# Order edges for inverses and output blocks, output blocks loaded a wave ahead, and a row of ones written once, in a two-layer RWKV-7 / attention backbone

## The chip, the cores and the metric

One NeuronCore of a Trainium2 chip. The metric is the device time of one execution in microseconds, lower is better. The kernel before took 2486.58 us in the median of 3 runs (2473.8 to 2494.9). All data is float32; products that need its precision are made of two or three matmuls on a rounded high part and a low part.

## The reference, cut to what matters

Two layers work on 1280 tokens (256 of context, 1024 latent) of width 1024. A layer projects the modulated stream into three groups of heads, lets each group mix the tokens, multiplies with a gate, projects back and normalises. Group A is a recurrence over the tokens that runs in both directions:

```python
def _rwkv7_step(S, inp):
    r, w, k, v, kk, b = inp
    sa = jnp.einsum('bhvk,bhk->bhv', S, kk)
    S = S * w[:, :, None, :] - sa[..., None] * b[:, :, None, :] + v[..., None] * k[:, :, None, :]
    return S, jnp.einsum('bhvk,bhk->bhv', S, r)
...
    yn = ((ys - mu) * lax.rsqrt(var + GN_EPS)).reshape(T, B, RWKV_W) * gn_g + gn_b
    bonus = jnp.sum(jnp.sum(r[:, :, None] * kd * r_k, axis=-1, keepdims=True), axis=2) * v
```

Groups B (grouped-query attention) and C (attention in a window of a grid) are softmax attention:

```python
        s = jnp.einsum('bqgrd,bsgd->bgrqs', qi, keys).astype(jnp.float32)
        p = jax.nn.softmax(s, axis=-1).astype(vals.dtype)
        return jnp.einsum('bgrqs,bsgd->bqgrd', p, vals)
...
    y_l = jnp.concatenate([yr_l * jax.nn.silu(rg_l), ya_l * jax.nn.silu(ag_l),
                           yn_l * jax.nn.silu(ng_l)], axis=-1) @ w_out
```

## The kernel before, in words

**Stages of a layer.** `layer_proj` projects; `rwkv` (L512, group A) is started in its middle; `attention` (L808, groups B and C) and `out_weights` / `out_proj` follow. They are traced one after the other, but the order in which an engine carries them out is drawn up when the kernel is built: `TileContext` is opened with `schedule_with_timeline_sim=True`, and its planner fills each engine's queue from the traced instructions by their order of tracing and by its own idea of when each becomes ready. On the chip each queue is then followed as it stands. So the attention, traced later, fills what the recurrence leaves free. `follow` (L803) gives the planner an edge without a semaphore: an instruction may not stand ahead of another one. It is used for one matmul in `weigh` (L924).

**The recurrence by waves.** The 1280 tokens make `NW` = 10 waves of 128, a wave 4 steps of 32 tokens, both directions at once. For each wave there are six stages of preparation and one chain:

- `p` `wave_pre` (L545): loads r, kk, kd, bd from DRAM (L556, tags `ldr` with 2 buffers, `ldkk`, `ldkd`, `ldbd` with 1), decays (tiles `th`, `iv`, `lp`), products into `G` and `kb`.
- `g` `wave_gram` (L602): Gram matrices (L610) and masks (L615). `l` `wave_low` (L590): their lower triangles go to DRAM `ls_d` (L594) and come back spread out as `lin` (L600).
- `i` `wave_inv` (L631): two copies from `lin` to `nn` (L634, L635), 15 steps of two dependent VectorE operations each (L643, L645), then through DRAM `inv_d` (L656, L660) into `di`. `k` `wave_kt` (L618): transposes. `m` `wave_merge` (L663): two rounds of small matmuls (L674) and `tt` (L679).
- `wave_chain` (L682): per step loads of v into one of three `X` tiles (L696), clearing of X (L698), matmuls (L703), a copy (L706), matmuls (L714), copies (L720), matmuls into the state (L724) and the update that writes the next X (L729). The step's output (`out_step`, L742, tile `py`) is put off to behind the next step's copy. After a wave its outputs go to DRAM `y_d` (L749).

`out_block` (L755) takes 128 tokens once both directions have written them: 7 loads (L761 y, L764 yb in four pieces, L765, L766), the sum on GpSimd (L767), normalisation on VectorE, ScalarE and GpSimd (L769 to L776), three transposes into PSUM (L780, tile `pso`), scale and shift (L782), bonus (L785), gate (L786), store to `yg_d` (L787), which `out_proj` reads (L1130). y and yb share the two buffers of `ldr`; the odd block of a pair takes `th` and `iv` for its other two tiles, the even one `ldkd` and `ldbd`. PSUM of the tag `pp` (two buffers) holds `psz`, `pcu`, `gt`, `kt`, `mg`, `py` and `pso` alike.

The order of tracing is the loop at L790: `wave_chain(w)`, then stages i, k of wave w+2, p, g, l of w+3, m of w+2, then output blocks: from wave 6 on the pair (11 - w, w), and in layer 0 the pair (0, 1) after wave 1.

**Attention.** `load_k` (L833) loads a head's keys twice (L830), rounds them (`k1`, L837), takes the rest on GpSimd into rows 0 to 63 of `k2` (L838), and writes a row of ones into row 64 (L839), which the correction matmul (L937) uses to add the row of maxima. It is called 6 times a layer. Scores (L867) give maxima (L869, L871, L874); then scores again (L936, L937), exponentials (L943, L946), sums (L950, L955) and the product with v (L921).

Of the kernel before, what the change touches and what calls it, by code (L numbers as in the profile page):

```python
# [8 lines left out]
F32 = mybir.dt.float32  # L9
F32R = mybir.dt.float32r  # L10
AF = mybir.ActivationFunctionType
ALU = mybir.AluOpType
AX = mybir.AxisListType
# [4 lines left out]
T = 1280  # L18
# [25 lines left out]
def body(tc, a):  # L44
    nc = tc.nc
# [10 lines left out]
    ident = cload("ident", [128, 128], nc.gpsimd)  # L56
# [444 lines left out]


# [9 lines left out]
    def rwkv(l, lay):  # L512
        last = l == DEPTH - 1
# [8 lines left out]
        z = bank[:, 0:384].rearrange("p (d c v) -> p d c v", d=2, c=3)  # L522
# [20 lines left out]
        pend = []  # L543

# [86 lines left out]
        def wave_inv(w):  # L631

            nn = r2.tile([128, 16, 16], F32, tag="nn", name="nn")
            nc.vector.tensor_copy(nn[0:64], lin[0:64].rearrange("p i t -> p t i"))  # L634
            nc.vector.tensor_copy(nn[64:128], lin[64:128])  # L635
# [46 lines left out]
        def wave_chain(w):  # L682
# [5 lines left out]
            for j in range(4):  # L688
# [3 lines left out]
                for d in range(2):  # L692
                    t0 = 128 * wave_block(w, d) + 32 * jc[d]
                    for p in range(2):
                        q, qs = QV[d][p], QSA[d][p]
                        nc.sync.dma_start(out=x[q:q + 32, d, :, p, :],  # L696
                                          in_=vt_d[t0:t0 + 32, :].rearrange("t (c e v) -> t c e v", c=3, e=2)[:, :, p, :])
                        nc.gpsimd.memset(x[qs:qs + 32, d, :, p, :], 0.0)  # L698
# [27 lines left out]
                if s < 4 * NW - 1:  # L726
                    for p in range(2):
                        o = slice(64 * p, 64 * p + 64)
                        nc.vector.tensor_tensor(out=xn[o, :, :, p, :], in0=z[o], in1=dcj(dc[o, 0, j], j), op=ALU.mult)  # L729
# [22 lines left out]
        def dcj(v, j):  # L752
            return bass.AP(tensor=v.tensor, offset=v.offset, ap=[v.ap[0], [21 - 6 * j, 2], [1, 3], [0, 64]])

        def out_block(b, odd):  # L755
            t4 = ("th", "iv") if odd else ("ldkd", "ldbd")
            y, yb = (r3.tile([128, 6, 64], F32, tag=t, name="yo", bufs=2) for t in ("ldr", "ldr"))
            bv, gt = (r3.tile([128, 3, 128], F32, tag=t, name="go", bufs=1) for t in t4)
            hv = lambda t: t.rearrange("p h v -> p (h v)")
# [7 lines left out]
            nc.gpsimd.tensor_tensor(out=y, in0=y, in1=yb, op=ALU.add)  # L767
            sm = r3.tile([128, 2, 6], F32, tag="sm", name="sm")
            nc.vector.tensor_reduce(out=sm[:, 0], in_=y, op=ALU.add, axis=AX.X)  # L769
# [19 lines left out]
        stages = dict(p=wave_pre, g=wave_gram, l=wave_low, i=wave_inv, k=wave_kt, m=wave_merge)  # L789
        for w in range(-3, NW):  # L790
            if w >= 0:
                wave_chain(w)
            for c in "ikpglm":
                v = w + (2 if c in "ikm" else 3)
                if 0 <= v < NW:
                    stages[c](v)
            for i, b in enumerate((11 - w, w) if w > 5 else (0, 1) if w == 1 and not last else ()):
                out_block(b, i)
        for f in pend:
            f()  # L800
        es.close()

    def follow(ins, prev):  # L803

        tc.add_manual_dep(ins.ins, prev.ins.name, mybir.DependencyInfo(mybir.DependencyClass.NoSync, mybir.DependencyReason.DATA), reason="order")


    def attention(l):  # L808
# [13 lines left out]
        nl = [0]  # L822

# [9 lines left out]
        def load_k(h):  # L833
            sg_ = dup(k_d[h])
            k1 = ap2.tile([128, T], F32R, tag="k1", name="k1")
            k2 = ap2.tile([65, T], F32R, tag="k2", name="k2")
            nc.scalar.copy(k1, sg_)  # L837
            nc.gpsimd.tensor_tensor(out=k2[0:64, :], in0=sg_[0:64, :], in1=k1[0:64, :], op=ALU.subtract)  # L838
            nc.vector.tensor_scalar(out=k2[64:65, :], in0=sg_[64:65, :], scalar1=0.0, scalar2=1.0, op0=ALU.mult, op1=ALU.add)  # L839
            return k1, k2  # L840
# [551 lines left out]
```

## Time and profile before

| | |
|---|---|
| median of 3 runs | 2486.58 us |
| the profiled execution | 2487.74 us |
| its span, first to last instruction | 2485.9 us |
| TensorE busy | 2207.0 us (89%) |
| VectorE busy | 1644.2 us (66%) |
| GpSimd busy | 1183.7 us (48%) |
| ScalarE busy | 1004.3 us (40%) |
| mean granted TensorE clock | 0.936 |
| DMA | 298.17 MB, mean 120 GB/s |

Engines in the profile: PE is TensorE's matmuls, PEld its weight loads, DVE VectorE, ACT ScalarE, POOL GpSimd; SPq is the queue of SyncE, which issues nearly all DMAs. L12 is line 12 of the kernel. In a timeline a row has the start (us), the duration, engine, line, operation, out<-in, and in brackets the engine's idle time before it and what ended it. In a row of waits stand the one that waited, what it waited for, the sum in us, the number of times and the longest. A row of busy times of a stretch has, behind its length, the busy time and the number of instructions of PE, PEld, DVE, ACT and POOL, the granted clock (1 is full speed), the DMA share and GB/s. TensorE's busy time is modelled at its ends, and at a lower clock the same work shows as more busy time.

### The profile page before, as it was taken

The numbers are of one execution on the slowest core, as the hardware profiler recorded it, in microseconds if no ns is written. First come the engines' busy times: TensorE is split into PE (matmuls) and PEld (weight loads), VectorE is DVE, ScalarE is ACT, GpSimd is POOL, SyncE is SP. The second block draws the span as 40 slices with busy tenths as digits, with TensorE's granted clock in tenths as the row PEclk, the third lists the DMA queues.
The fourth block names the chain that finished last, engine by engine and source line by source line (L and its number), as shares of the span: only waits on it lengthen the run. The fifth ranks groups of instructions, "written<-read, shape, count | busy, mean of one in ns | idle before, by whom it ended". The sixth has DMA issues, their size and how long they took to land.

```text
span 2485.9 us, 57805 instructions
## 1 busy us (share of the span) xinstructions
PE 2207.0 (89%) x22616; PEld 1648.8 (66%) x22616; DVE 1644.2 (66%) x3071; ACT 1004.3 (40%) x2186; POOL 1183.7 (48%) x1438
## 2 busy tenths in 40 slices
PE   6999999996898888889899999999868889999797
PEld 3777898774455555545797777787645656555497
DVE  5686433545867778767487796624568878877746
ACT  3333413334453545445233434214344545554522
POOL 3464425335454545344345365433455655645432
PEclk9999999996898989899999999999978989999899
DMA  7344334446554444334332455335564544332332
GB/s 273 114 155 165 119 90 118 124 109 145 129 119 111 96 98 114 101 89 140 110 100 80 140 168 181 110 91 122 132 138 112 122 106 111 96 81 67 115 111 92
DMA packets 448241, 298.17 MB, mean 120 GB/s; under 512 B 249600, under 2 KB 395880, under 8 KB 446944
## 3 DMA queue, kind: packets, MB, share of 16 engines
q1 hardware_dynamic: 439936, 281.71, 41.6%
q0 software_dynamic: 7392, 10.28, 1.5%
q8 instruction: 178, 2.92, 0.5%
q10 hardware_dynamic: 640, 2.49, 0.4%
q14 instruction: 95, 0.78, 0.1%
HBM read 198.37 MB, written 91.79 MB: 117 GB/s over the span
## 4 chain that ended last, share of the span: by engine, by line
PE 43%; DVE 22%; DMA 15%; issue 7%; ACT 5%; POOL 4%; SPq 4%; DVEq 0%; POOLq 0%; ACTq 0%
PE pj L204 5%; PE pj L203 5%; PE pj L205 5%; PE y L921 3%; DMA yf<-yg_d 2%; PE sm L867 2%; DVE G L615 2%; DMA ls_d<-G 2%; PE st L936 2%; DVE tmp L643 2%; DVE mx L869 2%; PE st L937 2%; DVE e L645 2%; PE ch L724 1%; DMA lin<-ls_d 1%
## 5 line engine op out<-in xcount | busy, mean ns | idle before, releaser
L204 PE MATMUL pj<-hlo,wh 128*128 128x512 f32 (+1 forms) x1072 | 402.0, 375 | 12.0 <-DVE hlo L480 7.3
L203 PE MATMUL pj<-hhi,wh 128*128 128x512 f32 (+1 forms) x1072 | 402.2, 377 | 9.1 <-ACT qr L348 5.2
L205 PE MATMUL pj<-hhi,wl 128*128 128x512 f32 (+1 forms) x1072 | 400.0, 374 | 0.2 <-POOL wl L169 0.2
L204 PEld LDWEIGHTS pj<-hlo,wh 128*128 128x128 f32 x1072 | 204.9, 191 | 54.3 <-DVE hlo L480 7.5
L203 PEld LDWEIGHTS pj<-hhi,wh 128*128 128x128 f32 x1072 | 204.0, 191 | 53.6 <-issue 6.8
L169 POOL TENSOR_TENSOR wl<-wf,wh 128x512 fp32r<-128x512 f32 x104 | 142.2, 1372 | 203.6 <-ACT wh L168 188.7
L869 DVE TENSOR_REDUCE mx<-sm 128x1 f32<-128x512 f32 (+1 forms) x372 | 198.9, 553 | 56.6 <-PE sm L867 54.9
L205 PEld LDWEIGHTS pj<-hhi,wl 128*128 128x128 f32 x1072 | 204.7, 191 | 38.1 <-issue 3.2
L943 ACT ACTIVATE pt<-st 128x512 f32<-128x512 f32 (+1 forms) x292 | 165.6, 582 | 144.2 <-PE st L937 141.6
L921 PE MATMUL y<-pt,v 128*64 128x256 f32 (+1 forms) x1392 | 220.0, 408 | 1.3 <-ACT pt L946 1.3
L867 PE MATMUL sm<-k,q 128*128 128x256 f32 (+2 forms) x436 | 169.1, 425 | 26.2 <-DVE mx L869 14.2
L936 PE MATMUL st<-q,k 128*128 128x512 f32 (+3 forms) x376 | 169.0, 452 | 24.0 <-ACT pt L943 8.0
L1159 PE MATMUL pj<-yh,wh 128*128 128x256 f32 x576 | 162.7, 291 | 8.1 <-ACT yh L1133 5.0
L1160 PE MATMUL pj<-yl,wh 128*128 128x256 f32 x576 | 165.5, 290 | 0.9 <-POOL yl L1134 0.8
L1161 PE MATMUL pj<-yh,wl 128*128 128x256 f32 x576 | 162.9, 287 | 0.0
L921 PEld LDWEIGHTS y<-pt,v 128*64 128x64 f32 x1392 | 96.6, 146 | 93.0 <-issue 64.5
L950 POOL TENSOR_TENSOR acc<-acc,pt 128x512 f32<-128x512 f32 x80 | 105.9, 1324 | 95.1 <-ACT pt L943 94.7
L937 PE MATMUL st<-q,k 65*128 65x512 f32 (+3 forms) x376 | 149.3, 400 | 1.1 <-ACT q L881 1.1
L867 PEld LDWEIGHTS sm<-k,q 128*128 128x128 f32 x436 | 82.4, 202 | 92.5 <-DVE mx L869 29.1
L615 DVE TENSOR_TENSOR G<-gt,msk 64x192 f32<-64x192 f32 (+1 forms) x320 | 110.4, 345 | 36.0 <-PE gt L610 24.8
L698 POOL MEMSET X<- 32x192 f32 x320 | 81.7, 255 | 102.2 <-PE py L742 75.7
L950 DVE TENSOR_TENSOR acc<-acc,pt 128x512 f32<-128x512 f32 x112 | 114.7, 1034 | 16.9 <-ACT pt L943 14.9
(276 smaller groups left out, 5124.8 us busy)
## 6 DMA issues: line engine op xcount, KB each, us to landing
wf<-win SPq DMA_DIRECT2D x104, 256.0 KB
wm<-wmod SPq DMA_DIRECT2D x32, 512.0 KB
yf<-yg_d SPq DMA_DIRECT2D x72, 128.0 KB
wt<-wm SPq DMA_DIRECT2D x8, 1024.0 KB
gate_d<-o SPq DMA_DIRECT2D x32, 256.0 KB
wf<-wout SPq DMA_DIRECT2D x16, 512.0 KB
ldkk<-rw_d SPq DMA_DIRECT2D x40, 192.0 KB
ldkd<-rw_d SPq DMA_DIRECT2D x40, 192.0 KB
```

The source lines that it names most:

```text
L203: nc.tensor.matmul(out=ps[:, :n], lhsT=wh, rhs=hhi[:, k, t0:t0 + n], start=(k == 0), stop=False)
L204: nc.tensor.matmul(out=ps[:, :n], lhsT=wh, rhs=hlo[:, k, t0:t0 + n], start=False, stop=False)
L205: nc.tensor.matmul(out=ps[:, :n], lhsT=wl, rhs=hhi[:, k, t0:t0 + n], start=False, stop=(k == KT - 1))
L867: nc.tensor.matmul(out=sp_[:, :o], lhsT=q[0][:, qc:qc + 128], rhs=k[0][:, c0:c0 + o], start=True, stop=True)
L869: nc.vector.tensor_reduce(out=mx[:, n_:n_ + 1], in_=sp_[:, :o], op=ALU.max, axis=AX.X)
L921: mm = nc.tensor.matmul(out=y[64 * i:64 * i + 64, a0:a1], lhsT=v[:, t, :], rhs=pt[:, p0:p0 + a1 - a0], start=start, stop=stop and at == le ...
L936: nc.tensor.matmul(out=o, lhsT=k[0][:, 128 * t:128 * t + 128], rhs=q[0][:, qa:qb], start=True, stop=False)
L937: mm = nc.tensor.matmul(out=o, lhsT=k[1][0:65, 128 * t:128 * t + 128], rhs=q[1][0:65, qa:qb], start=False, stop=True)
L943: nc.scalar.activation(out=pt[:, :w], in_=sp_[:, :w], func=AF.Exp)
L950: eng.tensor_tensor(out=acc[i][:, :w], in0=sums[i][:, :w], in1=pt[:, :w], op=ALU.add)
L1160: nc.tensor.matmul(out=p_, lhsT=wh[m][:, k], rhs=yl, start=False, stop=False)
L1161: nc.tensor.matmul(out=p_, lhsT=wl[m][:, k], rhs=yh, start=False, stop=(x_ == KT - 1))
```

## The change

Three things, in the same launch with the same arithmetic:

1. Each chain notes its second step's update on VectorE and its last clearing of X on GpSimd (`mark`). The two first copies of each inverse (VectorE) and the first GpSimd and first VectorE operation of each output block get an edge, by `follow`, behind the note of the chain traced last.
2. `out_block` is split into `out_load` and `out_block`. Loads are traced at the end of a wave's round, their compute in the next round, between `wave_chain` and the stages. The odd block of a pair has y and yb in the buffers of `ldkk` and `lp`. The blocks 0 and 1 of layer 0 load one at a time, after waves 1 and 2; the last pair of a layer computes after the loop.
3. The two `k2` tiles are taken once per layer from the pool without rotation, and their rows of ones are written there, from the constant `ident`; `load_k` alternates between them and writes rows 0 to 63 alone.

```diff
+        mark = {}
+
+        def behind(ins, eng):
+
+            if eng in mark:
+                follow(ins, mark[eng])
...
-            nc.vector.tensor_copy(nn[0:64], lin[0:64].rearrange("p i t -> p t i"))
-            nc.vector.tensor_copy(nn[64:128], lin[64:128])
+            behind(nc.vector.tensor_copy(nn[0:64], lin[0:64].rearrange("p i t -> p t i")), "v")
+            behind(nc.vector.tensor_copy(nn[64:128], lin[64:128]), "v")
...
-                        nc.gpsimd.memset(x[qs:qs + 32, d, :, p, :], 0.0)
+                        ms = nc.gpsimd.memset(x[qs:qs + 32, d, :, p, :], 0.0)
...
-                        nc.vector.tensor_tensor(out=xn[o, :, :, p, :], in0=z[o], in1=dcj(dc[o, 0, j], j), op=ALU.mult)
+                        up = nc.vector.tensor_tensor(out=xn[o, :, :, p, :], in0=z[o], in1=dcj(dc[o, 0, j], j), op=ALU.mult)
+                    if j == 1:
+                        mark.update(v=up, g=ms)
...
-        def out_block(b, odd):
+        def out_load(b, odd):
             t4 = ("th", "iv") if odd else ("ldkd", "ldbd")
-            y, yb = (r3.tile([128, 6, 64], F32, tag=t, name="yo", bufs=2) for t in ("ldr", "ldr"))
+            if odd:
+                y, yb = r3.tile([128, 6, 64], F32, tag="ldkk", name="yo", bufs=1), r2.tile([128, 6, 64], F32, tag="lp", name="yo")
+            else:
+                y, yb = (r3.tile([128, 6, 64], F32, tag="ldr", name="yo", bufs=2) for _ in range(2))
...
-            nc.gpsimd.tensor_tensor(out=y, in0=y, in1=yb, op=ALU.add)
+            return ts_, y, yb, bv, gt
+
+        def out_block(ts_, y, yb, bv, gt):
+            behind(nc.gpsimd.tensor_tensor(out=y, in0=y, in1=yb, op=ALU.add), "g")
             sm = r3.tile([128, 2, 6], F32, tag="sm", name="sm")
-            nc.vector.tensor_reduce(out=sm[:, 0], in_=y, op=ALU.add, axis=AX.X)
+            behind(nc.vector.tensor_reduce(out=sm[:, 0], in_=y, op=ALU.add, axis=AX.X), "v")
...
+        waiting, loaded = [], []
         for w in range(-3, NW):
             if w >= 0:
                 wave_chain(w)
+            for f in loaded:
+                out_block(*f)
+            loaded = []
             for c in "ikpglm":
                 v = w + (2 if c in "ikm" else 3)
                 if 0 <= v < NW:
                     stages[c](v)
-            for i, b in enumerate((11 - w, w) if w > 5 else (0, 1) if w == 1 and not last else ()):
-                out_block(b, i)
+            waiting += (11 - w, w) if w > 5 else (0, 1) if w == 1 and not last else ()
+            for i in range(2 if w > 5 else 1):
+                if waiting:
+                    loaded.append(out_load(waiting.pop(0), i))
         for f in pend:
             f()
+        for f in loaded:
+            out_block(*f)
         es.close()
...
+        k2s = [ap1.tile([65, T], F32R, tag=f"k2{i}", name=f"k2{i}") for i in range(2)]
+        for z in k2s:
+            nc.vector.tensor_scalar(out=z[64:65, :], in0=ident[64:65, 0:64].unsqueeze(2).to_broadcast([1, 64, 20]), scalar1=0.0, scalar2=1.0, op0=ALU.mult, op1=ALU.add)
+        nk = [0]
...
-            k2 = ap2.tile([65, T], F32R, tag="k2", name="k2")
+            k2 = k2s[nk[0] % 2]
+            nk[0] += 1
...
-            nc.vector.tensor_scalar(out=k2[64:65, :], in0=sg_[64:65, :], scalar1=0.0, scalar2=1.0, op0=ALU.mult, op1=ALU.add)
```

More of the change, by code (lines that the diff above doesn't have):

```diff
@@ L500, in lowrank, with follow @@
         return dict(zw=zw, aw=aw)
+    def follow(ins, prev):
+        tc.add_manual_dep(ins.ins, prev.ins.name, mybir.DependencyInfo(mybir.DependencyClass.NoSync, mybir.DependencyReason.DATA), reason="order")
     QSA = ((32 * 3, 32 * 1), (32 * 2, 32 * 0))
@@ L753, in dcj @@
             return bass.AP(tensor=v.tensor, offset=v.offset, ap=[v.ap[0], [21 - 6 * j, 2], [1, 3], [0, 64]])
-        def out_block(b, odd):
+        hv = lambda t: t.rearrange("p h v -> p (h v)")
+        def out_load(b, odd):
             t4 = ("th", "iv") if odd else ("ldkd", "ldbd")
-            y, yb = (r3.tile([128, 6, 64], F32, tag=t, name="yo", bufs=2) for t in ("ldr", "ldr"))
+            if odd:
+                y, yb = r3.tile([128, 6, 64], F32, tag="ldkk", name="yo", bufs=1), r2.tile([128, 6, 64], F32, tag="lp", name="yo")
+            else:
+                y, yb = (r3.tile([128, 6, 64], F32, tag="ldr", name="yo", bufs=2) for _ in range(2))
             bv, gt = (r3.tile([128, 3, 128], F32, tag=t, name="go", bufs=1) for t in t4)
-            hv = lambda t: t.rearrange("p h v -> p (h v)")
             ts_ = slice(128 * b, 128 * b + 128)
@@ L796, in rwkv @@
                     stages[c](v)
-            for i, b in enumerate((11 - w, w) if w > 5 else (0, 1) if w == 1 and not last else ()):
-                out_block(b, i)
+            waiting += (11 - w, w) if w > 5 else (0, 1) if w == 1 and not last else ()
+            for i in range(2 if w > 5 else 1):
+                if waiting:
+                    loaded.append(out_load(waiting.pop(0), i))
         for f in pend:
             f()
+        for f in loaded:
+            out_block(*f)
         es.close()
-    def follow(ins, prev):
-        tc.add_manual_dep(ins.ins, prev.ins.name, mybir.DependencyInfo(mybir.DependencyClass.NoSync, mybir.DependencyReason.DATA), reason="order")
     def attention(l):
```

## The prediction

> **What bounds the kernel now.** The views were read in this order: the page's totals, the busy times by stage, the timelines of single engines where the recurrence stands still, the waits.
>
> ```profile
> span 2485.9 us, 57805 instructions
> 600.00:1197.00 597.00, 515.48 (x6995) 321.87 (x6996) 448.60 (x1039) 290.08 (x698) 294.33 (x373) 0.91 0.44 111
> 1800.00:2359.00 559.00, 478.33 (x6935) 306.55 (x6935) 439.85 (x1026) 275.26 (x641) 305.00 (x385) 0.91 0.44 106
> ```
>
> The span is 2485.9 us; the profiled execution as a whole took 2487.74 us, and the sum below is made against that. It is 1.2 us above the median of the three runs, 2486.58 us, which spread from 2473.8 to 2494.9; so a measurement of this kernel can tell about 1% (25 us) from no change. The second and third rows are the stretches, 597 and 559 us long, in which the recurrence and the attention share the engines; the columns are the length, the busy time of TensorE, its weight loads, VectorE, ScalarE and GpSimd, then the granted clock. TensorE is busy for 86% of both, at a mean clock of 0.91. That is where a change of order can win: TensorE's idle time and its lost clock there. Below, the "full-clock work" of a stretch is TensorE's busy time times the granted clock, divided by the length.
>
> Three single steps of the chain are far too long. For each of them the rows show the matmuls of the third step (L724), the next transposes of an output block (L780) and the update that ends the step (L729); for the first also the output step (L742). The columns are start, duration, engine and line, and at the end the idle time before and what ended it.
>
> ```profile
> 628.16 0.91 PE L724 MATMUL ch<-X,S 128*64 128x64 f32 x22
> 685.13 0.55 PE L780 MATMUL pso<-c_ident,yo 128*128 128x128 f32 x3
> 685.61 0.54 PE L742 MATMUL py<-X,G 128*32 128x64 f32 x24
> 686.25 1.14 DVE L729 TENSOR_TENSOR X<-ch,dc 64x384 f32<-64x384 f32 x2 [1.34 <-PE py L742]
> 984.88 0.92 PE L724 MATMUL ch<-X,S 128*64 128x64 f32 x24 [1.98 <-DVE nm L874]
> 1029.85 0.84 PE L780 MATMUL pso<-c_ident,yo 128*128 128x128 f32 x3
> 1031.57 1.14 DVE L729 TENSOR_TENSOR X<-ch,dc 64x384 f32<-64x384 f32 x2 [0.79 <-PE py L742]
> 2176.33 0.92 PE L724 MATMUL ch<-X,S 128*64 128x64 f32 x24 [2.01 <-DVE X L720]
> 2196.06 0.49 PE L780 MATMUL pso<-c_ident,yo 128*128 128x128 f32 x3
> 2197.12 1.14 DVE L729 TENSOR_TENSOR X<-ch,dc 64x384 f32<-64x384 f32 x2 [0.17 <-PE py L742]
> ```
>
> From the matmuls to their update pass 57, 46 and 20 us, 123 us in all (the last two matmuls of the first group came 1.2 us behind the rest). Each time the update is released by L742, and L742 follows L780 of the second of two output blocks. The update overwrites an X that an earlier output step still reads; that output step is queued on TensorE behind the block's transposes, and these wait for the block. The second block is late because it loads into the buffers of the first:
>
> ```profile
> 629.34 1.00 POOL L767 TENSOR_TENSOR yo<-yo 128x384 f32<-128x384 f32 x1 [2.75 <-DMA yo<-y_d]
> 658.46 0.38 SPq L787 DMA_DIRECT2D yg_d<-yo  x1
> 661.65 1.74 SPq L764 DMA_DIRECT2D yo<-y_d  x4
> SPq L761 <- DVE yo L776: 64.6, 9, 11.8
>   POOL X L698: 75.7, 22
> ```
>
> The first block works from 629.3 to its store at 658.5; only at 661.7 the rest of the second block's loads go out, and it needs until 685.1 to reach its transposes. In the whole run SP's queue stood 64.6 us before L761 until the previous block was done with its squares (L776), and GpSimd stood 75.7 us before memsets of X that wait for output steps (the last row: who waited for py), with attention's additions queued behind.
>
> What the stalls cost is less than their length, since attention fills them. It is what TensorE does less than right behind them:
>
> ```profile
> 628.00:686.00 58.00, 47.99 (x485) 26.57 (x483) 48.24 (x141) 24.50 (x50) 26.83 (x23) 0.88 0.55 134
> 686.00:760.00 74.00, 63.91 (x984) 41.83 (x976) 51.33 (x126) 38.48 (x96) 39.77 (x54) 0.92 0.56 126
> 985.00:1031.00 46.00, 38.93 (x314) 22.21 (x318) 38.42 (x88) 16.28 (x31) 18.46 (x14) 0.85 0.33 81
> 1031.00:1097.00 66.00, 62.99 (x1044) 39.05 (x1036) 46.51 (x91) 36.23 (x92) 32.12 (x51) 0.97 0.38 107
> 2176.00:2197.00 21.00, 17.31 (x108) 9.96 (x108) 15.67 (x45) 7.31 (x16) 6.85 (x6) 0.76 0.32 72
> 2197.00:2297.00 100.00, 97.11 (x1339) 58.66 (x1336) 73.25 (x140) 57.26 (x132) 52.51 (x67) 1.00 0.29 76
> ```
>
> Full-clock work in the three stalls: 47.99 x 0.88 / 58 = 0.73, 38.93 x 0.85 / 46 = 0.72, 17.31 x 0.76 / 21 = 0.63. Behind them: 63.91 x 0.92 / 74 = 0.79, 62.99 x 0.97 / 66 = 0.93, 97.11 / 100 = 0.97. The deficits are 0.06 x 58 + 0.21 x 46 + 0.34 x 21 = 4 + 9 + 7 = 20 us.
>
> **The change, part by part.**
>
> (1) Output blocks are traced behind the next chain and load a wave ahead. Each block's 7 DMA issues (126 for 18 blocks) go out a wave before its compute and stand on SP before the next chain's X loads; in exchange SP no longer waits within a pair, since the odd block has buffers of its own (ldkk, lp). The compute comes behind the next chain's second step, on VectorE and GpSimd by an edge, and its transposes behind that chain's output steps. So the three long waits should go: **-20 us**. Bounds: 0, if the same work is only displaced, and -123 us, if the chain set the end. I take 20, near the former, because the chain doesn't set it:
>
> ```profile
> L724 PE MATMUL ch<-X,S x960: 219/222/370, 470.6 to 1152.1; 128*64 128x64 f32 x192
> L1159 PE MATMUL pj<-yh,wh x132: 279/283/582, 1196.7 to 1249.8; 128*128 128x256 f32 x132
> 685.75 0.38 SPq L556 DMA_DIRECT2D ldr<-rw_d  x1
> ```
>
> Layer 0's chain ends at 1152.1, and the output projection, which waits for attention, starts at 1196.7. What hides the moved blocks is attention on TensorE; without that cover, in the last pair, a block costs what it costs today. Queued behind the blocks are now the same wave's inverse, transposes, gram and merge, which were ahead of them; their results are due a wave or more later, so I take 0 for that, and it returns in the slow bound of (2). Wave 5's loads of r need the buffers that block 0 now holds early; today they go out even later, at 685.8 in the third row, because they wait for block 1.
>
> (2) The order edges on inverses bind only where L634 stands ahead of the second step's update today.
>
> ```profile
> 975.82 1.12 DVE L729 TENSOR_TENSOR X<-ch,dc 64x384 f32<-64x384 f32 x2
> 983.10 1.02 DVE L634 COPY nn<-lin 64x256 f32<-64x256 f32 x1
> 2160.06 0.38 DVE L634 COPY nn<-lin 64x256 f32<-64x256 f32 x1 [0.77 <-DMA lin<-ls_d]
> 2160.37 1.11 DVE L729 TENSOR_TENSOR X<-ch,dc 64x384 f32<-64x384 f32 x2
>   DMA lin<-ls_d: 72.5, 26
> ```
>
> Paired by wave, 13 of the 16 inverses with a mark lie behind it already, like the first pair; three lie ahead, like the second, at most by 5 us (1924.7 against 1929.7). The edge is an order in VectorE's queue and no wait of its own. So I take 0. Bounds: +15 us, if each of the three comes 5 us late for a merge that a chain waits for, and -36 us, half of the 72.5 us that VectorE stands before L634 and L635 for lin, if the new order gives those loads time.
>
> (3) The row of ones: 12 writes become 4, at the start of attention, and no longer wait for the k load.
>
> ```profile
> L839 DVE TENSOR_SCALAR k<-stg 1x1280 fp32r<-1x1280 f32 x12 | 16.6, 1386 | 4.6 <-DMA stg<-k_d 4.3
> 559.14 0.82 DVE L839 TENSOR_SCALAR k<-stg 1x1280 fp32r<-1x1280 f32 x1 [1.24 <-DMA stg<-k_d]
> 635.97 2.88 POOL L838 TENSOR_TENSOR k<-stg,k 64x1280 fp32r<-64x1280 f32 x1
> 636.78 2.76 DVE L839 TENSOR_SCALAR k<-stg 1x1280 fp32r<-1x1280 f32 x1
> 673.77 3.02 DVE L839 TENSOR_SCALAR k<-stg 1x1280 fp32r<-1x1280 f32 x1
> ```
>
> VectorE spends 16.6 us on them; four at 0.82 us leave 3.3, so 13 us go. Two of the long ones, 2.76 and 3.02 us, lie in the first stall, where VectorE is busy for 48.24 of 58 us. I take **-6 us**, those two; bounds 0 and -13. The Trainium skill, "SBUF — State Buffer", section "Who interferes with whom", says that VectorE and GpSimd hold a shared port pair exclusively: the second to issue is blocked until the first is done, also when the VectorE instruction has two SBUF inputs. The trace agrees: 0.82 us alone, 2.76 beside a GpSimd subtraction of 2.88. By this rule the blocked time would pass on to the next VectorE instruction with two inputs, so only 8 x 0.82 = 6.6 us of VectorE's time would go, not 13.
>
> (4) The ends. The last pair's loads go out together, not one after the other.
>
> ```profile
> 2376.49 1.86 PE L1159 MATMUL pj<-yh,wh 128*128 128x256 f32 x7 [4.76 <-ACT yh L1133]
> 1159.00:1172.00 13.00, 11.85 (x59) 5.63 (x60) 9.99 (x16) 11.54 (x20) 5.26 (x3) 1.00 0.81 259
> 2318.00:2359.00 41.00, 28.96 (x141) 14.19 (x139) 29.62 (x35) 23.23 (x41) 18.68 (x11) 0.83 0.45 145
> ```
>
> In layer 1 the output projection stands for 4.8 us before 2376.5 because its inputs, fetched through SP, come late beside the last block's loads and store: **-5 us**, bounds 0 and -10 with the same in layer 0.
>
> (5) The price. A chain that ends earlier, by up to 123 us in all, leaves that much of attention with no recurrence beside it. Alone and before its drain (second row) it works at 11.85 x 1.00 / 13 = 0.91, mixed at 0.93 and 0.97, middle 0.95: 123 x 0.04 = **+5 us**; bounds 0 and the slow rival's +47.
>
> Sum: 2487.7 - 20 - 6 - 5 + 5 = **2462 us**.
>
> **The rivals.**
>
> *The stalls were full already.* TensorE's work is the same in sum, and attention only comes at other times. For: TensorE is still busy for 83, 85 and 82% of the stalls, as in the whole stretches (86%). Against: the clock in the stalls, 0.76 to 0.88. Then only the ones count: 2487.7 - 6 = 2482 us.
>
> *Attention alone starves (slower).* With the chain gone early, attention's last heads run at the rate of the drain, where TensorE waits for each exponential and each sum: 28.96 x 0.83 / 41 = 0.59 in the third row of (4), against 0.97 mixed. 123 x 0.38 = 47 us are lost; nothing of the 20 and the 5 is won, and the ones give 6: 2487.7 + 47 - 6 = 2529 us. It decides once attention alone works at less than 0.97 - 31/123 = 0.72, where the loss eats up all gains. Against: the 0.91 before the drain.
>
> *The held inverses pay.* The 36 us of (2) come on top of the other gains: 2462 - 36 = 2426 us. For: VectorE, busy for 448.60 of the 597 us, is the fullest engine beside TensorE, and what it stands for lin is idle time at the head of its queue. Against: 13 of 16 lay behind the mark already. That the edges do nothing, so that this part of the change does not do what it says, is the forecast's own view.
>
> **How the numbers follow.** Forecast 0.56, its own range 2440 to 2480; full stalls 0.20; starved attention 0.13; paying inverses 0.11. Faster by 1% is below 2486.6 - 24.9 = 2461.7, so half of the forecast's cases, 0.29 (the unknown bounds lie a little more on that side), and the paying inverses: 0.40. The other 0.27 and the full stalls are within 1%: 0.47. Slower: 0.13. The range 2430 to 2500 holds the forecast and the full stalls and reaches towards both other cases; it leaves out some 0.18.
>
> **What would show it.** Right: no step with over 30 us from L724 to its update; SP no longer standing before L761 for L776; GpSimd's wait for output steps well below 75.7 us; L839 gone, and 4 writes of about 0.8 us in its place; layer 0's chain ending well before 1152; full-clock work of 0.8 or more where the stalls were. Wrong: output steps again behind transposes in waves 7 to 9; chains that wait for a merge (L674) because an inverse came late; attention below 0.72 between the end of the chain and the first L1159; chain ends that do not move.

## The result, and the profile after

The changed kernel takes 2469.03 us (median of 19 runs, 2459.3 to 2480.8), the kernel before 2485.16 us (19 runs beside them): a ratio of 0.9936, interval 0.9921 to 0.9952, 0.6% or 16 us faster. The profiled executions, 2478.6 and 2487.7 us, show 9 us of it; the one after was 9.6 us above its median, the one before 2.6 above its own. So what follows compares two single executions.

The long waits are gone. The longest from L734 (L724 before) to its update is 12.2 us, against 56. The page after opens with these totals:

```profile
span 2476.9 us, 57781 instructions
PE 2189.6 (88%) x22616; PEld 1645.0 (66%) x22616; DVE 1625.1 (66%) x3063; ACT 1003.5 (41%) x2186; POOL 1184.1 (48%) x1438
```

In the timelines of TensorE and VectorE these are the third steps that the prediction showed, wave 2 and wave 7 of layer 0 (L734 the matmuls, in wave 7 only the last ten, L739 the update, L799 a block's transposes). The last two rows are of the second step of wave 8 (L788 a block's sum):

```profile
625.89 0.92 PE L734 MATMUL ch<-X,S 128*64 128x64 f32 x24
636.76 1.13 DVE L739 TENSOR_TENSOR X<-ch,dc 64x384 f32<-64x384 f32 x2
648.73 0.90 PE L799 MATMUL pso<-c_ident,yo 128*128 128x128 f32 x3
...
933.48 0.56 PE L734 MATMUL ch<-X,S 128*64 128x64 f32 x10
942.10 1.13 DVE L739 TENSOR_TENSOR X<-ch,dc 64x384 f32<-64x384 f32 x2
...
989.57 1.12 DVE L739 TENSOR_TENSOR X<-ch,dc 64x384 f32<-64x384 f32 x2 [2.30 <-PE ch L734]
990.72 0.55 DVE L788 TENSOR_REDUCE sm<-yo 128x6 f32<-128x384 f32 x1
```

A block's transposes (648.7) no longer stand between the third step's matmuls (625.9) and its update (636.8), but behind both. What is left there are 9.9 us in wave 2 and 8.1 us in wave 7; before these updates VectorE has no idle time (their rows have no brackets), so they stand behind other work in VectorE's queue. The last two rows fit the order edge: the block's sum (L788) starts right behind the update of a second step. Layer 0's chain now ends at 1060, not 1152, and the four writes of ones take 0.8 to 1.8 us (the lines' instructions: count, shortest, median and longest, first and last start):

```profile
L734 PE MATMUL ch<-X,S x960: 216/222/370, 469.3 to 1060.2; 128*64 128x64 f32 x192
L848 DVE TENSOR_SCALAR k<-c_ident x4: 819/1269/1797, 547.1 to 1779.8; 1x1280 fp32r<-1x1280 f32 x4
```

The first row here is layer 0 with the recurrence; the other two are attention alone, behind the chain's end in each layer, where TensorE is busy for 57.34 of 67 and 34.84 of 37 us (stretches, columns as in the prediction):

```profile
600.00:1060.00 460.00, 400.76 (x6309) 263.98 (x6308) 348.28 (x895) 228.76 (x579) 243.68 (x333) 0.91 0.49 117
1060.00:1127.00 67.00, 57.34 (x352) 30.64 (x348) 52.50 (x91) 36.62 (x69) 41.48 (x28) 0.92 0.54 169
2297.00:2334.00 37.00, 34.84 (x201) 18.34 (x201) 28.91 (x47) 24.21 (x47) 15.17 (x12) 1.00 0.50 145
```

GpSimd's wait for output steps, 75.7 us before, has not moved:

```profile
  POOL X L708: 74.6, 21
```

What the time went into is read from the two stretches from the last projection matmul to the last output matmul, layer 0 and layer 1. The columns are the stretch, its length, the busy time of TensorE, weight loads, VectorE, ScalarE and GpSimd, the granted clock, DMA share and GB/s. The page's totals of before, then its stretches:

```profile
PE 2207.0 (89%) x22616; PEld 1648.8 (66%) x22616; DVE 1644.2 (66%) x3071; ACT 1004.3 (40%) x2186; POOL 1183.7 (48%) x1438
```

```profile
545.60:1327.90 782.30, 670.91 (x8587) 465.86 (x8586) 565.43 (x1217) 346.94 (x813) 378.02 (x468) 0.90 0.45 114
1788.20:2464.10 675.90, 584.98 (x7836) 410.18 (x7835) 502.31 (x1089) 305.93 (x708) 343.45 (x442) 0.91 0.43 107
```

and after:

```profile
545.60:1315.40 769.80, 667.51 (x8589) 470.42 (x8587) 550.30 (x1214) 346.96 (x813) 377.97 (x468) 0.90 0.46 116
1778.20:2457.10 678.90, 572.25 (x7835) 401.74 (x7835) 501.42 (x1086) 305.21 (x708) 342.61 (x442) 0.92 0.43 106
```

Length less busy time is TensorE's idle time: in layer 0 it falls from 111.4 to 102.3 us, in layer 1 it rises from 90.9 to 106.6. TensorE's busy time for the same 22616 matmuls falls by 17.4 us (2207.0 to 2189.6), 12.7 of it in layer 1. So the span's 9.0 us are 17.4 us of faster matmuls less 8.4 us of more idle time. (no_inv_edges, below, is nearly the same program; its profile has 2200.2 us, 6.8 below before, and 574.1 in layer 1. So the drop in layer 1 comes again, 10.9 us there, the rest does not.) One new wait makes up for all that was won in idle time (SP's and TensorE's timeline at the end of layer 1, after):

```profile
2341.05 1.09 SPq L1033 DMA_DIRECT2D yg_d<-gtl  x2
2344.13 3.00 SPq L1281 DMA_DIRECT2D s<-x_d  x3
2347.17 11.61 SPq L1157 DMA_DIRECT2D yf<-yg_d  x4
2356.49 0.74 ACT L1160 CAST yh<-yf 128x256 fp32r<-128x256 f32 x2 [12.38 <-DMA yf<-yg_d]
2356.94 1.86 PE L1186 MATMUL pj<-yh,wh 128*128 128x256 f32 x7 [17.15 <-ACT yh L1160]
```

Attention ended 16.0 us earlier (2333.8 against 2349.8), the first output matmul came only 2.2 us earlier (2356.9 against 2359.1). Ahead of the fetches of yf the planner now has the three loads of s, 1 MB each; the first cast had to wait 12.4 us for its fetch, and TensorE stood for 17.2 us. From 2346 to 2355 the DMAs moved 345 GB/s without a gap. Before, four of the eight fetches went ahead of the loads of s.

### The profile page after: what moved, and what is told of

The parts are those of the page before. It is cut to its first block, busy times and chain, and to the rows that moved or that the text cites. A ratio compares the mean times of both kernels' runs of the same rounds, so it can differ in the third digit from the quotient of the medians.

```text
span 2476.9 us, 57781 instructions
## 1 busy us (share of the span) xinstructions
PE 2189.6 (88%) x22616; PEld 1645.0 (66%) x22616; DVE 1625.1 (66%) x3063; ACT 1003.5 (41%) x2186; POOL 1184.1 (48%) x1438
## 4 chain that ended last, share of the span: by engine, by line
PE 44%; DVE 21%; DMA 15%; issue 7%; ACT 6%; POOL 4%; SPq 3%; DVEq 0%; POOLq 0%; ACTq 0%
PE pj L203 5%; PE pj L204 5%; PE pj L205 5%; PE y L948 4%; DMA yf<-yg_d 3%; PE st L963 3%; PE sm L894 3%; DMA ls_d<-G 3%; DVE G L625 2%; PE st L964 2%; DVE mx L896 2%; DVE tmp L653 2%; PE ch L734 2%; PE py L754 1%; DMA lin<-ls_d 1%
## 5 line engine op out<-in xcount | busy, mean ns | idle before, releaser
L948 PE MATMUL y<-pt,v 128*64 128x256 f32 (+1 forms) x1392 | 211.5, 398 | 2.3 <-ACT pt L973 1.4
L708 POOL MEMSET X<- 32x192 f32 x320 | 81.2, 254 | 102.0 <-PE py L754 74.6
L1186 PEld LDWEIGHTS pj<-yh,wh 128*128 128x128 f32 x576 | 109.9, 196 | 26.0 <-ACT yh L1160 23.5
```

What stands on the lines that cost most here:

```text
L948: mm = nc.tensor.matmul(out=y[64 * i:64 * i + 64, a0:a1], lhsT=v[:, t, :], rhs=pt[:, p0:p0 + a1 - a0], start=start, stop=stop and at == le ...
L1186: nc.tensor.matmul(out=p_, lhsT=wh[m][:, k], rhs=yh, start=(x_ == 0), stop=False)
```

## The experiments

Each run has its ratio to the kernel before on the same chip (medians of before there: 2481.5 us for the first four runs of the table behind after, 2481.1 for ones_only to mark_third, 2486.9 for the last four). The wait is the longest from a step's matmuls to its update; "all waits" is their sum over the 78 updates. Idle 0 and 1 are TensorE's idle time in the two stretches as above, the gap is its idle time between attention's last product with v and layer 1's first output matmul. Waits, idle times and gap come from one profiled execution of each kernel, the ratio from all of its runs.

| kernel | us | ratio (95%) | wait | all waits | idle 0 | idle 1 | gap |
|---|---|---|---|---|---|---|---|
| before | 2485.2 | 1 | 56.0 | 291 | 111 | 91 | 6 |
| after | 2469.0 | 0.9936 (0.9921–0.9952) | 12.2 | 163 | 102 | 107 | 21 |
| no_inv_edges | 2469.8 | 0.9951 (0.9930–0.9973) | 11.5 | 161 | 101 | 99 | 21 |
| no_block_edges | 2480.6 | 1.0004 (0.9987–1.0022) | 12.0 | 149 | 98 | 95 | 5 |
| no_ones | 2461.9 | 0.9928 (0.9900–0.9956) | 15.6 | 163 | 93 | 89 | 0 |
| end_order | 2461.3 | 0.9920 (0.9894–0.9945) | 11.2 | 158 | 100 | 87 | 9 |
| ones_only | 2506.5 | 1.0112 (1.0081–1.0142) | 51.9 | 297 | 108 | 117 | 30 |
| buffers_only | 2488.3 | 1.0038 (1.0015–1.0061) | 32.2 | 238 | 94 | 104 | 23 |
| shared_buffers | 2483.1 | 1.0014 (0.9990–1.0038) | 14.9 | 165 | 99 | 94 | 7 |
| mark_third | 2445.8 | 0.9862 (0.9830–0.9895) | 12.5 | 109 | 90 | 88 | 12 |
| ones_end | 2503.8 | 1.0061 (1.0038–1.0085) | 51.9 | 293 | 107 | 107 | 23 |
| mark_third_end | 2451.0 | 0.9848 (0.9818–0.9878) | 12.7 | 107 | 93 | 86 | 12 |
| mark_first_end | 2468.9 | 0.9929 (0.9903–0.9954) | 13.0 | 149 | 102 | 79 | 4 |
| mark_fourth_end | 2496.7 | 1.0035 (1.0013–1.0058) | 28.7 | 204 | 91 | 119 | 16 |

The theory at the start was the prediction's: the removed stalls give the gain, the ones a little. The rivals: VectorE's relief by the ones; the edges; and that the planner, which orders the whole program anew after any edit, merely found a better order.

**no_inv_edges.** The edges on L644 and L645 taken out.

```
-            behind(nc.vector.tensor_copy(nn[0:64], ...), "v")
-            behind(nc.vector.tensor_copy(nn[64:128], lin[64:128]), "v")
+            nc.vector.tensor_copy(nn[0:64], ...)
+            nc.vector.tensor_copy(nn[64:128], lin[64:128])
```

> The changed kernel without the order edges on the inverses' first copies (L644, L645). In the queues it differs from the changed kernel by one single swap: in one wave a copy of lin stands ahead of the second step's update again. My theory (the gain comes from the three removed stalls of the chain) and the rival that the ones' 16.6 us of VectorE made it both expect the time of the changed kernel, 2469 us, within 3 us. A theory that the inverse edges carry the gain expects 2475 to 2485.

The interval overlaps that of the changed kernel, as both theories had it: no effect of the inverse edges is seen (by the ratios 4 us, give or take 7). As the program differs by one swap, this is also a second profile of the same order: 2474.0 against 2476.9, TensorE busy for 574.1 against 572.3 us in layer 1, but for 2200.2 against 2189.6 in the whole.

**no_block_edges.** The edges on L786 and L788 taken out.

```
-            behind(nc.gpsimd.tensor_tensor(out=y, in0=y, in1=yb, op=ALU.add), "g")
-            behind(nc.vector.tensor_reduce(out=sm[:, 0], ...), "v")
+            nc.gpsimd.tensor_tensor(out=y, in0=y, in1=yb, op=ALU.add)
+            nc.vector.tensor_reduce(out=sm[:, 0], ...)
```

> The changed kernel without the order edges on the output block's first addition and first sum; the blocks are still loaded a wave ahead into buffers of their own and traced behind the chain. If the removed stalls came from the loads and buffers alone, the longest wait of a step for its update stays below 30 us and the time within 4 us of 2469. If the edges are what keeps the blocks' transposes from standing in front of output steps, a wait of 20 us or more comes back and the time rises by 5 to 15 us.

A miss for both sides, and the one that brought the theory down: no wait above 12.1 us came back, and still the gain is gone. Its stretches:

```profile
547.40:1310.40 763.00, 665.13 (x8588) 467.78 (x8587) 548.82 (x1214) 347.38 (x813) 376.75 (x468) 0.91 0.46 117
1766.10:2449.10 683.00, 587.86 (x7835) 409.33 (x7835) 501.39 (x1085) 306.33 (x708) 344.81 (x442) 0.91 0.42 106
```

Idle time is below that of before in layer 0 (97.9 us) and about that of before in layer 1 (95.1); layer 1's matmuls are busy for 587.9 us, like before and 15.6 us above the changed kernel's. (The profiled run, 2472.7, was the fastest of its 12; the ratio goes by all of them.)

**no_ones.** The ones written at each k load again.

```
-            k2 = k2s[nk[0] % 2]
-            nk[0] += 1
+            k2 = ap2.tile([65, T], F32R, tag="k2", name="k2")
...
+            nc.vector.tensor_scalar(out=k2[64:65, :], in0=sg_[64:65, :], ...)
```

> The changed kernel with the row of ones written at every k load again (12 writes of together about 16.6 us on VectorE). My theory expects 2469 plus the 6 us that the prediction gave to this part, 2472 to 2478. The rival that relief of VectorE made the gain expects 2480 to 2486, about the time before. A third, that neither matters much and the order that the planner finds decides, allows a change of either sign of up to 8 us.

Not slower: 0.9928, where a loss of 6 us would be 0.996, just outside the interval. But the changed kernel's own ratio is uncertain too, and here the planner also left no gap at the end of layer 1 (0 against 21 us), which could hide a loss. Beside end_order, on the same chip and with a gap of 9, it is 2 us slower, give or take 9. So a loss of 6 us is neither seen nor excluded; the rival's 11 to 17 us are unlikely. The third line holds.

**end_order.** At the end of layer 1 the loads of s behind the fetches.

```
+            sl = nc.sync.dma_start(out=s, ...)
+            if last and x_ < 3:
+                follow(sl, first)
```

(first is the last of the eight fetches of the first block.)

> The changed kernel with one order more: at the end of layer 1 the three loads of s (1 MB each) stand on SP behind the eight fetches of yf for the first block, as they did (by the planner's choice) in the kernel before. Theory: TensorE's idle 17.2 us before the output projection of layer 1 (17.15 before 2356.94, released by a cast that had waited 12.4 us for the fetch) come from these 3 MB ahead of the fetch; the first output matmul then comes about 10 us earlier and the time is 2457 to 2463. Rival: the fetches are slow anyway, for they wait for the last head's store and the weights' loads, and the s loads then come late for the additions; no change, within 3 us of 2469.

As the theory had it, at 2461.3 us, though the interval (0.9894 to 0.9945) still touches that of no_inv_edges on the same chip (0.9930 to 0.9973). (The profiled run, 2448.3, was the fastest of its 6, 13 us below their median.) SP's and TensorE's timeline there:

```profile
2321.45 1.09 SPq L1033 DMA_DIRECT2D yg_d<-gtl  x2
2322.64 5.99 SPq L1157 DMA_DIRECT2D yf<-yg_d  x4
2325.04 0.81 ACT L1160 CAST yh<-yf 128x256 fp32r<-128x256 f32 x2 [0.56 <-DMA yf<-yg_d]
2325.50 1.86 PE L1187 MATMUL pj<-yh,wh 128*128 128x256 f32 x7 [4.87 <-ACT yh L1160]
```

From the last store to the first output matmul it now takes 4.1 us (2321.45 to 2325.50), before the repair 15.9 (2341.05 to 2356.94), and TensorE's wait is 4.9 instead of 17.2 us. The Trainium skill, "DMA: Bandwidth & Descriptors", section "Two DMAs through the same engine are not ordered", says that within one queue of a DMA engine descriptors start in order; the traces fit this: behind 3 MB of s the first cast came 9.3 us after the fetch was issued (2347.17 to 2356.49), ahead of them 2.4 us.

**ones_only.** The kernel before with the third part alone.

```
+        k2s = [ap1.tile([65, T], F32R, tag=f"k2{i}", ...) for i in range(2)]
+        for z in k2s:
+            nc.vector.tensor_scalar(out=z[64:65, :], ...)
...
-            nc.vector.tensor_scalar(out=k2[64:65, :], in0=sg_[64:65, :], ...)
```

> The kernel before with the third part alone: the row of ones written four times, at the start of attention, and output blocks and inverses as before. The prediction gave this part -6 us, bounds 0 and -13. The run without the ones showed no loss when they were left out, so the theory now is: no gain from it, 2478 to 2486 us, and the three long waits of the chain for output steps (57, 46 and 20 us) are still there in layer 0's waves 2 and 7. The rival (the ones give their 13 us of VectorE) expects 2468 to 2472.

Neither: 28 us by its ratio slower than before. The long waits are there as expected, and at the end of layer 1 the same leak as in the changed kernel, only larger:

```profile
628.25 0.92 PE L724 MATMUL ch<-X,S 128*64 128x64 f32 x24
679.43 0.55 PE L780 MATMUL pso<-c_ident,yo 128*128 128x128 f32 x3
681.10 1.13 DVE L729 TENSOR_TENSOR X<-ch,dc 64x384 f32<-64x384 f32 x2
...
2366.66 5.42 SPq L1258 DMA_DIRECT2D s<-x_d  x3
2372.18 2.73 SPq L761 DMA_DIRECT2D yo<-y_d  x1
2383.28 1.73 SPq L764 DMA_DIRECT2D yo<-y_d  x4
2386.28 3.77 SPq L1134 DMA_DIRECT2D yf<-yg_d  x3
2388.89 1.22 PE L1163 MATMUL pj<-yh,wh 128*128 128x256 f32 x4 [18.30 <-ACT yh L1137]
```

The loads of s (L1258) went out before the last block's own loads (L761, L764) and before the fetches; TensorE's first output matmul came at 2388.9, 32.6 us after attention's end at 2356.3.

**ones_end.** The same with the s loads behind the fetches, as in end_order.

> The kernel before with the third part (ones written four times), and with the three loads of s at the end of layer 1 behind the eight fetches of yf. The ones alone took 2506.5 us, 25 more than before, and their profile shows TensorE idle for 29.5 us between attention's end and the output projection of layer 1. Theory: what the ones alone cost is nearly all this idle stretch, made by s loads that the planner put ahead of the fetches; with the order put right the first output matmul follows attention's end within 12 us and the time is 2482 to 2490. Rival: the ones themselves, or the stalls that stay, cost the time; above 2498.

Better than the ones alone, 1.0061 against 1.0112, but 2503.8 us is above the theory's bound and where the rival had it, above 2498. The gap fell only from 29.5 to 22.9 us, for the last output block is itself late (the chain ends at 2339.8, after a wait of 35 us in wave 7), and its loads stand on SP ahead of the fetches:

```profile
2368.71 1.72 SPq L764 DMA_DIRECT2D yo<-y_d  x4
2370.54 4.52 SPq L1134 DMA_DIRECT2D yf<-yg_d  x4
```

So a stall that stays, longer here than in the kernel before (35 against 20 us), makes the end late, as the rival had it. Whether the ones have one too, the run doesn't tell apart.

**buffers_only.** The kernel before with ldkk and lp for the odd block.

```
+            if odd:
+                y, yb = r3.tile(..., tag="ldkk", ...), r2.tile(..., tag="lp", ...)
+            else:
+                y, yb = (r3.tile(..., tag="ldr", ...) for _ in range(2))
```

> The kernel before with the second block's own buffers alone (its y in ldkk and lp); blocks are still loaded and traced where they were, with no order edges. If SP's wait within a pair made the stalls, as the prediction said, SP no longer stands before the second block's first load for the first block's squares, the longest wait of a step for its update falls below 30 us, and most of the gain comes: 2468 to 2475. If the place in the program makes them, waits of 30 us and more stay and the time stays within 4 us of before, 2478 to 2486.

The waits fall from 56, 46 and 20 us to 32, 25 and 23 but stay, and nothing is gained (1.0038). The time is no clean test of the stalls: layer 0's idle time fell from 111 to 94 us, and a gap of 23 us at the end took that back. SP's wait within a pair was a part of the stalls, not all of their cause.

**shared_buffers.** The changed kernel with both blocks in ldr; the odd one is loaded behind the even one's work.

```
-            for f in loaded:
-                out_block(*f)
+            for i, f in enumerate(loaded):
+                out_block(*(f() if i else f))
...
```

> The changed kernel with both blocks of a pair in ldr again: the first is still loaded a wave ahead, the second is loaded only behind the first one's work; order edges and ones as changed. If the buffers matter, the second block's transposes come about 25 us behind the first one's and one or more waits of 20 us or longer between a step's matmuls and its update come back; the time is 2475 to 2485. If the loads ahead and the edges suffice, no wait above 20 us and a time within 4 us of the changed kernel's 2469.

SP again stood before blocks' loads for an earlier block's squares (from its waits: us, times, longest):

```profile
SPq L774 <- DVE yo L792: 49.6, 5, 12.9
```

and yet no step waited above 14.9 us: with the blocks traced behind the chain, loaded ahead and held by edges, the buffers aren't needed to remove the stalls. The time didn't follow: 1.0014. With no_block_edges this is the second kernel without stalls that isn't faster than before, and neither has a large gap at the end (7 and 5 us) that could hide a gain.

**mark_third, mark_third_end.** The mark at another step; the second with end_order's edge too.

```
-                    if j == 1:
+                    if j == 2:
                         mark.update(v=up, g=ms)
```

> The changed kernel with the mark at the third step's update instead of the second's: inverses and output blocks are held one step longer, some 12 to 15 us. If the place of the edge has a meaning (blocks behind the second step give the gain by their place), the later place costs or gives a steady few us that shows in the output blocks' times, and the stalls stay away; 2466 to 2474. If the gain of the edges is only one of many orders that the planner can find, this order may come out anywhere between 2455 and 2485 with the chain's waits no different from the changed kernel's.

> The kernel with the mark at the third step, which took 2445.8 us, with the loads of s behind the first block's fetches of yf. It has 12.1 us of idle TensorE between attention's end and layer 1's first output matmul, of which some 5 to 9 remain where the order is right. The theory of the end expects 2438 to 2444 us. If the order at the end is not what costs there, 2443 to 2449.

The fastest of all, 0.9862 and 0.9848, and 2445.8 us lies below both ranges expected of mark_third; 2451.0 us lies above both of mark_third_end, on a chip where before is slower by 6 us. The intervals of the two overlap, so nothing was seen of the end's order there (the gap is 12 us in both, for the planner had put only two fetches ahead of the s loads, and these two sufficed for the first matmuls). VectorE's timeline in wave 2 of layer 0 shows what the mark does:

```profile
623.97 1.12 DVE L739 TENSOR_TENSOR X<-ch,dc 64x384 f32<-64x384 f32 x2 [1.21 <-PE ch L734]
625.12 0.55 DVE L788 TENSOR_REDUCE sm<-yo 128x6 f32<-128x384 f32 x1
625.59 0.36 DVE L644 COPY nn<-lin 64x256 f32<-64x256 f32 x1
627.58 0.18 DVE L655 TENSOR_TENSOR e<-e,tmp 128x15 f32<-128x15 f32 x1
646.77 1.12 DVE L739 TENSOR_TENSOR X<-ch,dc 64x384 f32<-64x384 f32 x2 [2.10 <-PE ch L734]
```

The block's sum and the inverse now start right behind the third step's update, and the inverse's steps fill the time to the fourth. With the mark at the second step they lie in front of the third step's update, which is where that kernel's waits are: 103 of 163 us belong to the third step, here 41 of 109.

**mark_first_end, mark_fourth_end.** The same line with 0 and with 3, both with end_order's edge.

```
-                    if j == 1:
+                    if j == 3:
```

> The changed kernel with the mark at the first step's update and the s loads of layer 1's end behind the fetches. Together with no edges on blocks (2480.6 us), the second step (2461.3 with the same end) and the third (2445.8 without it) it asks whether the time falls with the step: a theory that the held work (inverse, sums of an output block) no longer stands on VectorE between a step's matmuls and its update expects 2464 to 2476, between none and second. If the order found by the planner is a matter of luck, it may be below 2461.

> The same with the mark at the fourth step's update, with the s loads behind the fetches: inverses and blocks are held to the end of the chain of a wave. If holding them longer keeps VectorE free for the chain, 2436 to 2450, as for the third step or below. If inverses then come late for the merges, chains wait for L684 and the time rises above 2455. If it is a matter of luck, anywhere from 2440 to 2480 with the chain's waits for updates no different.

The first step gives 0.9929, as the second does, and 2468.9 us is in the range of the theory, but nothing tells the two steps apart. The fourth gives 1.0035, far above what was expected of a VectorE kept free. With the fourth a stall is back, the longest waits being 24 and 29 us in layer 0 (TensorE's and VectorE's timeline):

```profile
691.07 0.92 PE L734 MATMUL ch<-X,S 128*64 128x64 f32 x24
710.03 1.15 PE L684 MATMUL mg<-di,G 32*32 32x32 f32 x96
713.38 0.74 PE L684 MATMUL mg<-di 32*32 32x32 f32 x62
715.40 0.54 PE L754 MATMUL py<-X,G 128*32 128x64 f32 x24
716.05 1.14 DVE L739 TENSOR_TENSOR X<-ch,dc 64x384 f32<-64x384 f32 x2
```

24.1 us pass from the matmuls to the update, since the output step (L754) stands on TensorE behind attention's work and the next merges (L684). TensorE was not idle before these merges, and the load of their inverse had gone out at 680.6, so it is the order on TensorE, and not an inverse that came late, which is shown. Why the planner put the merges there stays open. No run was made in which only one of the two block edges was left out.

## Why the prediction came close, and where it was wrong

2462 us was forecast, 2469 measured, in the range. But that the sum came so near was in good part luck, for most of its terms were not borne out by the runs.

**The stalls, -20 us.** That the three long waits go was right. That this is worth 20 us was not borne out, nor was the cause. By the prediction's own measure, TensorE's busy time times clock over length, where the stalls were:

```profile
628.00:686.00 58.00, 48.61 (x714) 34.00 (x716) 44.26 (x121) 29.70 (x75) 34.76 (x49) 0.79 0.57 129
985.00:1031.00 46.00, 42.59 (x687) 26.38 (x686) 32.97 (x64) 21.14 (x53) 22.00 (x34) 0.97 0.41 112
2160.00:2200.00 40.00, 34.54 (x591) 22.22 (x590) 37.03 (x93) 13.77 (x32) 22.09 (x29) 0.91 0.29 74
```

0.66, 0.90 and 0.79, where it was 0.73, 0.72 and 0.63: the first stall's stretch got worse (clock 0.79 instead of 0.88 at the same busy time), the second gained 0.18 x 46 = 8 us, the third 0.16 x 21 = 3; with the first's loss, 0.07 x 58 = 4, that is 7 us in all, and only roughly, as these stretches hold other work after than before. The bound of 0, "the same work is only displaced", fits the two kernels without stalls that gain nothing, no_block_edges and shared_buffers. The step that failed is "So the three long waits should go: -20 us", in its second half; of the cause, "since the odd block has buffers of its own" failed (shared_buffers).

**The edges on output blocks** were part of that term and had no price of their own. Without them the gain is gone (1.0004 against 0.9936), and one step later it is doubled; how far that is the edges' doing is told below.

**Inverse edges, 0:** right as far as no_inv_edges can tell. VectorE stands for lin for 66.4 + 13.9 = 80.3 us instead of 72.5 (its waits, after), so "the held inverses pay" is out.

```profile
DVE nn L645 <- DMA lin<-ls_d: 66.4, 16, 7.7
DVE nn L644 <- DMA lin<-ls_d: 13.9, 7, 3.5
```

**The ones, -6:** not seen in no_ones, ones_only or ones_end. VectorE's busy time does fall, by 14.8 us from no_ones to the changed kernel (1639.9 to 1625.1), and by 25.2 from before to ones_only. But it falls by 27.1 in buffers_only too (1644.2 to 1617.1), which still writes the row twelve times: a new order alone moves VectorE's total by as much. So these totals can't tell 13 us from the 6.6 us that the prediction worked out by the Trainium skill's shared port ("SBUF — State Buffer", section "Who interferes with whom"); and as buffers_only is no faster, VectorE's total isn't what decides.

**The ends, -5:** the wrong sign. The 4.8 us wait went, a 17.2 us one came in its place; the prediction looked at the last block's loads and store, not at the loads of s, which the planner moved. With their order put right the ratio is 0.9920 against the changed kernel's 0.9936, the right way but not clear of the noise.

**The price, +5:** none is seen in this kernel. Alone, attention works at 57.34 x 0.92 / 67 = 0.79 in layer 0 and 34.84 / 37 = 0.94 in layer 1; mixed with the recurrence, layer 0 works at 400.76 x 0.91 / 460 = 0.79 as well. The prediction's 0.95 for mixed work came from two good stretches behind stalls, not from the whole. Starved attention (below 0.72) is refuted; in layer 0 the planner also puts the first output matmuls beside the rest of attention (from 1126.9, before from 1196.7).

**Signs.** Right: the waits, the ones (though at 0.8 to 1.8 us each, not 0.8), the chain's end in layer 0, and SP, which no longer waits for an earlier block's squares before a block's loads. Wrong: GpSimd's wait for output steps, which was to fall well below 75.7 us and is 74.6, and the full-clock work of 0.8 or more, which one of the three stretches reaches.

**What remains.** Over the 14 profiles idle 0 and 1 together run from 178 to 225 us, and the span less this idle time from 2260 to 2290: idle time explains most of the spread, the granted clock a part of the rest. Beside the 23 runs of before with a median clock of 0.930, the 12 of no_inv_edges had 0.935. Five thousandths of some 2200 us busy are some 12 us by estimate, which is of the size of the gain. But no_ones (0.9305 beside 0.930) and mark_first_end (0.930 beside 0.929) gain as much (0.9928, 0.9929) without more clock, so it isn't the clock alone. Why some orders get more clock stays open.

What shorter waits are worth isn't settled either. Over the 14 kernels of the table the ratio rises with "all waits" (correlation 0.84; about 0.24 us of time for each us of wait), but every kernel has another order as well, several share nearly one, and no_block_edges and shared_buffers lie 16 and 17 us above that line.

Open, too, is how much of the block edges' effect is their place: the second step stands at 0.9920 to 0.9951 in four kernels, of which three share nearly one order, but at 1.0014 with shared buffers; the third step was run twice, in nearly one order. Orders that the planner finds differ by as much for edits that should not matter, as ones_only shows.

## What to carry to other kernels

A wait that is long in the profile isn't worth its length when other work fills it, and may not even be worth the deficit beside it: take the stall away in a cheap experiment that changes as little else as it can before you price it. Where a planner orders the program, any edit moves the order elsewhere, so look at the places where a few transfers stand in line at a stage's end, and pin down their order there by an edge; and when edges hold side work behind a chain, try each step of the chain as the mark.

## What the runs showed of the hardware

In the second of these two stretches of the changed kernel, 12 us each, the granted clock falls while TensorE is busy:

```profile
628.00:640.00 12.00, 9.49 (x318) 6.87 (x318) 11.77 (x28) 4.46 (x8) 6.60 (x8) 1.00 0.20 36
640.00:652.00 12.00, 10.67 (x74) 6.36 (x76) 9.73 (x31) 5.69 (x15) 6.08 (x14) 0.64 0.57 123
```

From 640 to 652 it was 0.64, with TensorE busy for 10.67 of 12 us and no idle time above 1.7 us in the whole of 628 to 686. The Trainium skill, "TensorE: Matmul & The Clock Gate", section "What's actually happening", ties the fall to an idle window of about 3.4 us; here that is not what is seen, and the measurement decides. Which matmuls bring the clock down was not tried.
